# The third feed-forward block by Strassen's algorithm, with sums of weights made by adding transfers

## The chip, the core and the metric

The kernel runs on one core of a Trainium2 chip. A core has five engines that run side by side, each with its own queue of instructions, taken in order: TensorE (PE, matrix products into PSUM banks), VectorE (DVE), ScalarE (ACT), GpSimd (POOL) and SyncE (SP, which issues transfers). Sixteen DMA engines carry the transfers, whoever issues them. The metric is the device time of one execution in microseconds; 1209.74 us is the median of three runs before the change (1209.62 to 1209.84).

## The reference

The model is a decoder trunk of two layers on 256 tokens of width 1024, all in float32. Each layer is

```python
h = _swiglu(x, ffn_w1[l, 0], ffn_w3[l, 0], ffn_w2[l, 0])
x = _layernorm(ALPHA * x + 0.5 * h, ln_g[l, 0], ln_b[l, 0])
h = _mixer(x, ...)                      # gated position mixing and differential attention
x = _layernorm(ALPHA * x + h, ln_g[l, 1], ln_b[l, 1])
h = _swiglu(x, ffn_w1[l, 1], ffn_w3[l, 1], ffn_w2[l, 1])
x = _layernorm(ALPHA * x + 0.5 * h, ln_g[l, 2], ln_b[l, 2])
```

with `_swiglu(x, w1, w3, w2) = (silu(x @ w1) * (x @ w3)) @ w2`. So there are four feed-forward parts, two a layer; `w1` and `w3` have 1024 rows and 2816 columns each. The change touches only the products `x @ w1` and `x @ w3`.

## The kernel before, in words

**Split products.** TensorE multiplies in a rounded float32 format. To keep precision, every operand is split in two: a high part (`hi`, the rounded value, made by a copy on ScalarE) and a low part (`lo`, the rest, made by a subtraction on VectorE). A product of two split operands is three matmuls, x_hi w_hi, x_hi w_lo and x_lo w_hi (`three`, L256), added up in one PSUM bank. Weights come from memory unsplit: `stream` (L152) loads 128x2048 numbers (1 MB) into a buffer `raw` (L163, issued by SyncE) and splits it (L178 on ScalarE, L180 on VectorE) into buffers of 128x1024, `whi` and `wlo`. There are four `raw` buffers and eight each of `whi` and `wlo`, so loads and splits run ahead of TensorE by as much as these hold.

**Blocks of a feed-forward.** `ffn` (L599) takes the columns of `w1` and `w3` in five blocks of 512 columns each of w1 and w3 (block n = 0 to 4), by `gemm_b2` (L317); the rest of the columns goes by another function, and then comes the product with `w2`. In `gemm_b2` the 256 tokens are two halves of 128 (t = 0, 1), the 1024 rows of the weights two halves c of 512, and m is 0 for w1 and 1 for w3: four 1 MB buffers of weights, 2 x 2 x 8 x 3 = 96 matmuls of 128x128 by 128x512 into four banks. First all of the weights with the first half of the tokens, then all again with the second, so the split weights of a block stay until its second half. After each half of the tokens `done` makes silu(w1 part) times the w3 part (L612 on ScalarE, L613 on VectorE) into `planes`, and a background task transposes it: GpSimd parts it into two planes of 16-bit numbers (L193), SyncE issues a transposing transfer (L197), GpSimd joins the planes (L202), and ScalarE and VectorE split the result (L629, L631) for the product with `w2`.

**The norm at the start.** The first feed-forward of the kernel has its input ready (`gemm_first`). The other three start while the layer norm before them ends: the class `Norm` scales, transposes (L573 to L580) and splits the tokens half by half during block 0, finishes the token rows (L541) during block 1, and these three are the stages with `norm` set.

**What sets the order.** TensorE's order is the order in which the program is written; `beat` counts its work in units of 12 matmuls, and background tasks (`beside`) are woken when a count is reached; `front` (L605) gives for each block how many units after its start a transposition is issued. For the other engines a scheduler fixes the order when the program is built, by priorities (`step` raises the number with each load, `soon` lowers it) and with `behind`, which puts an instruction after another one. In the run each engine then takes its instructions strictly in that order.

Of the kernel before, what the change touches and what calls it, by code (L numbers as in the profile page):

```python
# [54 lines left out]
def trunk(ctx, tc, x, xT, w13a, w13b, w2, wb, wqk, wu, wg, wgr, wbr, wbrr, wo, gateb, gatebr, sgug, sgub, sguwT, sgubias, lam, diffg,  # L55
# [93 lines left out]

        return tc.issue_after(ins) if ins is not None else nullcontext()  # L150

    def stream(src, width=CH, sub=HC, lent=(), after=(None, None), pool=()):  # L152

        step()
        raw = raw_pool.tile([P, CH], F32, tag="raw", name=name("raw"))
        for g in gate:
            g[0] -= 1
        while len(gate) > 1 and gate[1][0] < 0:  # L160
            gate.pop(0)
        with behind(gate[0][1] if gate and gate[0][0] < 0 else None):
            loaded[0] = nc.sync.dma_start(raw[:, :width], src).ins  # L163
        out = []
        first = sooner.pop() if sooner else latest
        for o in range(0, width, HC):
            eng = G if o // HC in pool else V
            if o // HC in lent:
                hi, lo = ([act.tile([P, 512], F32R, tag="slot", name=name(n)) for _ in range(2)] for n in ("lhi", "llo"))
                at = [(hi[j], lo[j]) for j in range(2)]  # L170
            else:
                hi = hi_pool.tile([P, HC], F32R, tag="hi", name=name("whi"))
                lo = lo_pool.tile([P, HC], F32R, tag="lo", name=name("wlo"))
                at = [(hi[:, p : p + sub], lo[:, p : p + sub]) for p in range(0, HC, sub)]
            for p, (h, w) in zip(range(0, HC, sub), at):
                r = raw[:, o + p : o + p + sub]
                with behind(first[0]):
                    A.activation(h, r, AF.Copy)  # L178
                with behind(after[o // HC] or (first[1] if eng is V else None)):
                    eng.tensor_tensor(out=w, in0=r, in1=h.bitcast(F32), op=ALU.subtract)  # L180
            out.append((hi, lo))
        return out
# [134 lines left out]
    def gemm_b2(srcs, xh, xl, done, norm=None, second=(0, 1), each=None):  # L317
# [9 lines left out]
        for t in range(NT):  # L327
# [14 lines left out]
            with behind(latest[0] if t == 0 else None):  # L342
                done(t, ps[t])

    def gemm_first(srcs, done):

        step()
# [89 lines left out]
    class Norm:  # L437
# [5 lines left out]

        def __init__(self, l, i, scale, eps, after, last=False):
            self.scale, self.eps, self.last, self.done, self.front = scale, eps, last, set(), i
            self.ends, self.xhi, self.xlo = [None] * NT, {}, {}
            self.gT, self.bT = (v[:, l, i] for v in (ln_g, ln_b))
            self.y = x_tok
            self.group = 256 if last else 512
            self.st = [sm("st", D // self.group * 6, bufs=2) for _ in range(NT)]  # L450
            self.g, self.b = bc_load(lng[l, i], after), bc_load(lnb[l, i], after)
            if last:
                A.activation(self.g, self.g, AF.Copy, scale=-0.5)
                self.minus = s512("minus")
                A.activation(self.minus[:, :P], ident, AF.Copy, scale=-1.0)
                self.eps_t = self.minus[:, 2 * P : 2 * P + 1]
                V.memset(self.eps_t, eps)
                with behind(silu[0]):
# [85 lines left out]
        def sent(self):  # L544

            two = [s512("ntwo")]
            with behind(loaded[0]):
                gate.append([3, moved(self.via[0], two[0])])
            yield 0.2
            self.affine(0, 1, self.via[0], self.via[0], (2, 2), two[0])  # L550
            with soon():
                for h in range(2):
                    self.plane(A, 1, h, 0)
            yield 0.4
            two += [s512("ntwo") for _ in range(2)]
            for h in range(2):
                last = moved(self.via[1 + h], two[1 + h])
            gate.append([2, last])
            yield 0.7
            self.affine(1, 0, self.via[1], self.via[1], (1, 1, 2), two[1])  # L560
            yield 1.7
            self.affine(1, 1, self.via[2], self.via[2], (2, 2), two[2])

        def affine(self, t, h, src, xf, pieces, two=None):
            self.done.add((t, h))
            k = 0
            with soon():
                for n in pieces:
# [17 lines left out]
            if (t, h) == (1, 1):  # L586
                latest[:] = last
                sooner.append((self.xhi[0, 1], self.xlo[1, 0]))

        def ready(self, t, h):  # L590
            assert (t, h) in self.done, (t, h)
# [7 lines left out]
    def ffn(l, f, i, norm, last=False):  # L599
# [33 lines left out]
        for n in range(NB):  # L633
            srcs = [w13b[l, f, m * NB + n] for m in range(2)]
            if n == 0 and norm is None:
                gemm_first(srcs, front(n, (10.3, 10.3)))
            else:
                gemm_b2(srcs, xh, xl, front(n, (13.3, 10.3)), norm=norm if n == 0 else None)
        for j in range(FA, FT - 4, 2):
            for m, z in gemm_a2([w13a[l, f, j - FA + m] for m in range(2)], both, lambda m: t512("silu")):  # L640
                s = z[:, :T]
# [403 lines left out]
```

## Time and profile before

| | |
|---|---|
| median of three runs | 1209.74 us |
| span of the profiled execution | 1208.3 us |
| TensorE busy | 1202.6 us, 5891 matmuls |
| VectorE busy | 903.2 us |
| ScalarE busy | 719.9 us |
| GpSimd busy | 332.9 us |
| read from memory | 236.52 MB, 197 GB/s over the span |

The time of the profiled execution itself is its span, from the first to the last instruction; the median of the runs is 1.4 us above it. In rows of the timeline the first number is the start in us from the start of the span, the second the duration of the group, then engine, line, operation, what is written from what is read, the count, and in brackets how long the engine had been idle and what ended that. In rows by group, the numbers behind the bar are busy time in us, mean duration in ns, and idle time before with what ended it. In rows on transfers the last number is the median time in us from issue to landing.

### The profile page before, as it was taken

How to read it: one execution, taken by the hardware profiler on the slowest of the kernel's cores; microseconds unless marked ns; L12 is line 12 of the kernel's file. 1: busy time of each engine (PE TensorE's matmuls, PEld its weight loads, DVE VectorE, ACT ScalarE, POOL GpSimd, SP SyncE). 2: the span in 40 equal slices, each digit the busy share in tenths (PEclk: the TensorE clock that was granted, in tenths of full speed). 3: DMA queues.
4: the chain of work that ended last, by engine and by line, in shares of the span. 5: the costliest groups of instructions: out<-in, count | busy, mean ns of one | idle time of the engine just before them, and what ended most of it. 6: DMA issues, size and time to landing. Idle time of an engine off the chain costs nothing.

```text
span 1208.3 us, 16816 instructions
## 1 busy us (share of the span) xinstructions
PE 1202.6 (100%) x5891; PEld 1013.3 (84%) x5891; DVE 903.2 (75%) x1544; ACT 719.9 (60%) x1388; POOL 332.9 (28%) x442
## 2 busy tenths in 40 slices
PE   9999999999999999999999999999999999999998
PEld 8888888888888888888888888888888888888887
DVE  6686669897689886766686756688966989776763
ACT  6465547668855665554555554576788556564740
POOL 1433101256421234330053330004464012423300
PEclk9999999999999999999999999999999999999999
DMA  9967646768765666767476766476676764877540
GB/s 347 303 219 238 253 174 203 259 200 231 240 213 180 200 231 208 249 201 261 149 245 198 259 187 261 148 273 238 211 205 199 251 192 153 274 231 239 186 181 35
DMA packets 124006, 263.58 MB, mean 218 GB/s; under 512 B 88417, under 2 KB 89489, under 8 KB 97809
## 3 DMA queue, kind: packets, MB, share of 16 engines
q1 hardware_dynamic: 119664, 248.80, 62.0%
q0 software_dynamic: 3824, 13.18, 3.4%
q8 instruction: 46, 0.75, 0.3%
q10 hardware_dynamic: 432, 0.52, 0.1%
q14 instruction: 40, 0.32, 0.1%
HBM read 236.52 MB, written 1.05 MB: 197 GB/s over the span
## 4 chain that ended last, share of the span: by engine, by line
PE 99%; DMA 0%; DVE 0%; ACT 0%; issue 0%; ACTq 0%
PE bank L256 72%; PE bank L268 15%; PE bank L275 8%; PE bank L374 2%; PE sbank L704 1%; PE sbank L760 1%; PE sbank L878 1%; DMA xraw<-in_xT 0%; PE sbank L758 0%; PE sbank L533 0%; PE sbank L512 0%; DVE xtok L520 0%; ACT whi L220 0%; DVE st L471 0%; DVE xtok L467 0%; ACT x L220 0%
## 5 line engine op out<-in xcount | busy, mean ns | idle before, releaser
L180 DVE TENSOR_TENSOR wlo<-raw,whi 128x512 fp32r<-128x512 f32 (+1 forms) x566 | 524.6, 962 | 114.8 <-ACT whi L178 80.0
L178 ACT ACTIVATE whi<-raw 128x512 fp32r<-128x512 f32 (+1 forms) x570 | 433.3, 799 | 246.6 <-PE bank L256 183.0
L256 PE MATMUL bank<-whi,x 128*128 128x512 f32 x1480 | 460.7, 390 | 0.0
L256 PEld LDWEIGHTS bank<-whi,x 128*128 128x128 f32 x1480 | 277.9, 188 | 57.7
L256 PE MATMUL bank<-wlo,x 128*128 128x512 f32 x740 | 288.0, 389 | 0.0
L256 PEld LDWEIGHTS bank<-wlo,x 128*128 128x128 f32 x740 | 139.0, 188 | 28.2
L268 PE MATMUL bank<-x,whi 128*128 128x512 f32 x640 | 153.3, 391 | 0.0
L256 PE MATMUL bank<-whi,hhi 128*128 128x512 f32 (+1 forms) x374 | 141.2, 378 | 0.0
L256 PE MATMUL bank<-wlo,hhi 128*128 128x512 f32 (+1 forms) x374 | 141.0, 377 | 0.0
L256 PE MATMUL bank<-whi,hlo 128*128 128x512 f32 (+1 forms) x374 | 140.9, 377 | 0.0
L193 POOL COPY planes<-planes 128x512 uint16<-128x512 uint16 x80 | 87.1, 1116 | 193.9 <-DVE planes L613 193.9
L268 PEld LDWEIGHTS bank<-x,whi 128*128 128x128 f32 x640 | 118.2, 188 | 23.8
L202 POOL COPY planes<-planes 128x512 uint16<-128x512 uint16 x80 | 70.9, 931 | 95.8 <-DMA planes<-planes 95.5
L613 DVE TENSOR_TENSOR planes<-planes,bank 128x512 f32<-128x512 f32 x40 | 27.4, 684 | 83.8 <-issue 69.3
L612 ACT ACTIVATE planes<-bank 128x512 f32<-128x512 f32 x40 | 23.9, 598 | 102.6 <-PE bank L256 101.5
L275 PEld LDWEIGHTS bank<-x,wlo 128*128 128x128 f32 x640 | 81.4, 191 | 2.9
L275 PE MATMUL bank<-x,wlo 128*128 128x256 f32 x640 | 82.6, 283 | 0.0
L256 PEld LDWEIGHTS bank<-whi,hlo 128*128 128x128 f32 x374 | 70.4, 188 | 13.0
L256 PEld LDWEIGHTS bank<-whi,hhi 128*128 128x128 f32 x374 | 70.4, 188 | 12.8
L256 PEld LDWEIGHTS bank<-wlo,hhi 128*128 128x128 f32 x374 | 70.4, 188 | 12.6
L575 POOL COPY nvia<-ntwo 128x256 uint16<-128x256 uint16 x20 | 10.4, 565 | 198.1 <-DMA ntwo<-nvia 179.9
L680 POOL TENSOR_TENSOR swap<-swap,sin_t 128x512 f32<-128x512 f32 x16 | 27.1, 1695 | 100.0 <-DMA swap<-z 78.0
(209 smaller groups left out, 1392.0 us busy)
## 6 DMA issues: line engine op xcount, KB each, us to landing
raw<-in_w13b SPq DMA_DIRECT2D x76, 1024.0 KB, 5.8
raw<-in_w SPq DMA_DIRECT2D x40, 1024.0 KB, 6.2
raw<-in_wb SPq DMA_DIRECT2D x16, 1024.0 KB, 5.1
raw<-in_wqk SPq DMA_DIRECT2D x16, 1024.0 KB, 6.3
raw<-in_w13a SPq DMA_DIRECT2D x8, 1024.0 KB, 5.1
raw<-in_wgr SPq DMA_DIRECT2D x8, 1024.0 KB, 5.3
raw<-in_wg SPq DMA_DIRECT2D x8, 1024.0 KB, 5.0
raw<-in_wu SPq DMA_DIRECT2D x8, 1024.0 KB, 6.4
```

Source lines behind the costliest of these rows:

```text
L178: A.activation(h, r, AF.Copy)
L180: eng.tensor_tensor(out=w, in0=r, in1=h.bitcast(F32), op=ALU.subtract)
L193: G.tensor_copy(out=planes(out)[:, w], in_=numbers(src)[:, w])
L202: eng.tensor_copy(out=numbers(out)[:, w], in_=planes(src)[:, w])
L256: PE.matmul(ps, xx, w, start=start and n == 0, stop=stop and n == 2)
L268: PE.matmul(b[-1], hi[:, k * P : (k + 1) * P], xc(k), start=k == 0, stop=False)
L275: PE.matmul(b[n][:, :T], lo[:, k * P : (k + 1) * P], xc(k)[:, :T], start=False, stop=k == KT - 1)
L374: PE.matmul(ps[t][m], x[:, j, o + t * P : o + (t + 1) * P], y, start=k0 + j == 0 and o == 0 and y is hi, stop=k0 + j == KT - 1 and y is lo)
L612: silu[0] = A.activation(s, ps[0], AF.Silu).ins
L613: added[0] = V.tensor_tensor(out=s, in0=s, in1=ps[1], op=ALU.mult).ins
L680: turned_by[0] = G.tensor_tensor(out=s3, in0=s3, in1=s, op=ALU.mult).ins
L704: PE.matmul(banks[m][:, j * nk : (j + 1) * nk], rows(qT, m, j, t * P, P), rows(kT, m, j, 0, nk), start=True, stop=True)
```

## The change

In the three feed-forwards that have a norm in front of them, block n = 2 goes by `gemm_seven` in place of `gemm_b2`. The block's product is one of 2 x 2 parts: the tokens' rows t and the input's columns c for x, the weights' rows c and w1 or w3 for w. With w11, w21 the two row halves of w1's columns and w12, w22 those of w3's, Strassen's algorithm in a form with seven products gives both outputs. Four of the products take a sum or difference of x parts, which `Norm.seven` forms and splits on VectorE and ScalarE after the last part of x is ready, and keeps in buffers `sum`. Four products take a sum of weights: the loaded `raw` buffer is first split as it is, and then a transfer issued by GpSimd adds another part into it (`gather`, two halves of 512 KB, `accum_op`), from memory (w12) or from another `raw` buffer (w22, w21), and it is split again. Each product is 12 matmuls; partial results are copied out of their banks (`kept`) and put together on VectorE. `fetch` is the front of `stream`, made a function of its own. For block 1 the count to its transposition is smaller by one unit, since the block behind it has one unit less.

```diff
+    def pieces(raw):
+        out = []
+        for o in range(0, CH, HC):
+            hi = hi_pool.tile([P, HC], F32R, tag="hi", name=name("whi"))
+            lo = lo_pool.tile([P, HC], F32R, tag="lo", name=name("wlo"))
+            split(hi, lo, raw[:, o : o + HC])
+            out.append((hi, lo))
+        return out
+
+    def gather(out, src):
+        for o in range(0, CH, HC):
+            G.dma_start(out[:, o : o + HC], src[:, o : o + HC], accum_op=ALU.add)
+
+    def gemm_seven(srcs, sums, done):
+        x11, x12, x22 = ((lambda k, o, h=h, t=t: x_cat[h][:, k, o + t * P : o + (t + 1) * P])
+                         for t, h in ((0, 0), (0, 1), (1, 1)))
+        s1, s2, s3, s4 = (lambda k, o, v=v: v[bool(o)][:, k * P : (k + 1) * P] for v in sums)
+        bx, by, bz = (side_bank() for _ in range(3))
+
+        def product(ps, x, w, first):
+            for k in range(KT // 2):
+                hi, lo = (v[:, k % 2 * 512 : k % 2 * 512 + 512] for v in w[k // 2])
+                for n, (y, o) in enumerate(((hi, 0), (lo, 0), (hi, T))):
+                    PE.matmul(ps, x(k, o), y, start=first and k == n == 0, stop=k == KT // 2 - 1 and n == 2,
+                              skip_group_check=True)
+                beat(0.25)
+
+        def kept(ps):
+            v = s512("part")
+            A.activation(v, ps, AF.Copy)
+            return v
+
+        (w11, w21), (w12, w22) = ((s[:, :CH], s[:, CH:]) for s in srcs)
+        r11 = fetch(w11)
+        product(bx, x11, pieces(r11), True)
+        gather(r11, w12)
+        product(bz, s1, pieces(r11), True)
+        a, z = kept(bx), kept(bz)
+        r22 = fetch(w22)
+        gather(r11, r22)
+        product(bx, s2, pieces(r11), False)
+        b = kept(bx)
+        r12 = fetch(w12)
+        gather(r12, r22)
+        product(bz, s4, pieces(r22), False)
+        r21 = fetch(w21)
+        product(bx, s3, pieces(r12), False)
+        c = kept(bx)
+        gather(r11, r21)
+        product(by, x12, pieces(r21), True)
+        V.tensor_tensor(out=a, in0=by, in1=a, op=ALU.add)
+        V.tensor_tensor(out=b, in0=bz, in1=b, op=ALU.subtract)
+        done(0, (a, b))
+        V.tensor_tensor(out=c, in0=z, in1=c, op=ALU.subtract)
+        product(bx, x22, pieces(r11), False)
+        done(1, (bx, c))
...
+            if self.front:
+                yield 4
+                yield from self.seven()
...
+        def seven(self):
+            x11, x12, x21, x22 = (self.rows[v] for v in ((0, 0), (0, 1), (1, 0), (1, 1)))
+            self.sums = [slots("sum", 4, F32R) for _ in range(4)]
+            for v, (out, a, b, op) in zip((0, 2, 1, 3), ((x22, x21, x22, ALU.subtract), (x21, x11, x21, ALU.subtract),
+                                                         (x11, x22, x11, ALU.subtract), (x12, x12, x11, ALU.add))):
+                V.tensor_tensor(out=out, in0=a, in1=b, op=op)
+                split(*self.sums[v], out)
+                yield 1
...
             if n == 0 and norm is None:
                 gemm_first(srcs, front(n, (10.3, 10.3)))
+            elif n == 2 and norm:
+                gemm_seven(srcs, norm.sums, front(n, (10.3, 10.3)))
             else:
-                gemm_b2(srcs, xh, xl, front(n, (13.3, 10.3)), norm=norm if n == 0 else None)
+                early = norm is not None and n == 1
+                gemm_b2(srcs, xh, xl, front(n, (13.3 - early, 10.3 - early)), norm=norm if n == 0 else None)
```

(`self.rows` keeps the rows of x that `affine` was given, for `seven`. The loads, `fetch`, are as in `stream` before.)

More of the change, by code (lines that the diff above doesn't have):

```diff
@@ L150, in behind, with fetch @@
         return tc.issue_after(ins) if ins is not None else nullcontext()
-    def stream(src, width=CH, sub=HC, lent=(), after=(None, None), pool=()):
+    def fetch(src, width=CH):
         step()
@@ L163, in stream @@
             loaded[0] = nc.sync.dma_start(raw[:, :width], src).ins
+        return raw
+    def stream(src, width=CH, sub=HC, lent=(), after=(None, None), pool=()):
+        raw = fetch(src, width)
         out = []
@@ L445, in __init__ @@
             self.scale, self.eps, self.last, self.done, self.front = scale, eps, last, set(), i
-            self.ends, self.xhi, self.xlo = [None] * NT, {}, {}
+            self.ends, self.xhi, self.xlo, self.rows = [None] * NT, {}, {}, {}
             self.gT, self.bT = (v[:, l, i] for v in (ln_g, ln_b))
@@ L562, in sent @@
             self.affine(1, 1, self.via[2], self.via[2], (2, 2), two[2])
+            if self.front:
+                yield 4
+                yield from self.seven()
         def affine(self, t, h, src, xf, pieces, two=None):
             self.done.add((t, h))
+            self.rows[t, h] = xf
             k = 0
```

## The prediction

> **What bounds the kernel now.** I read the page first (busy shares, the granted clock, the chain that ended last), then the busy times of one feed-forward block, then by engine the timeline around that block, and last the transfers.
>
> ```profile
> PE 1202.6 (100%) x5891; PEld 1013.3 (84%) x5891; DVE 903.2 (75%) x1544; ACT 719.9 (60%) x1388; POOL 332.9 (28%) x442
> PEclk9999999999999999999999999999999999999999
> PE 99%; DMA 0%; DVE 0%; ACT 0%; issue 0%; ACTq 0%
> ...
> PE sbank L386 <- DVE warm L382: 1.1, 1, 1.1
> ...
> core 0: us, PE busy (x) PEld busy (x) DVE busy (x) ACT busy (x) POOL busy (x), PEclk, DMA share, GB/s
> ...
> 466.42:488.18 21.76, 21.76 (x97) 18.02 (x96) 14.10 (x23) 11.31 (x23) 6.59 (x8) 1.00 0.67 230
> ```
>
> TensorE is busy all the time, at full granted clock, and the chain is 99% TensorE: its longest wait, at the start, is 1.1 us. So a matmul taken away is worth its full slot, and any wait put in front of one costs its full length. The last row is the third block of the feed-forward after the first mixer: 96 matmuls in 21.76 us, 0.2267 us each. I call this the first stage; the second is the next feed-forward (third block from 646.87), the third is the last one (from 1063.87). Block starts come from the SiLU rows below: SiLU starts when the first rows' w1 part is complete, which is 12 matmuls (2.72 us) before the middle of a block, so the next block starts 13.60 us later: 452.82 + 13.60 = 466.42.
>
> ```profile
> 452.82 0.60 ACT L612 ACTIVATE planes<-bank 128x512 f32<-128x512 f32 x1 [7.01 <-PE bank L256]
> 456.90 1.15 ACT L178 ACTIVATE whi<-raw 128x512 fp32r<-128x512 f32 x2 [3.48 <-PE bank L256]
> 633.27 0.60 ACT L612 ACTIVATE planes<-bank 128x512 f32<-128x512 f32 x1 [7.01 <-PE bank L256]
> 637.35 1.15 ACT L178 ACTIVATE whi<-raw 128x512 fp32r<-128x512 f32 x2 [3.48 <-PE bank L256]
> 1050.27 0.60 ACT L612 ACTIVATE planes<-bank 128x512 f32<-128x512 f32 x1 [7.01 <-PE bank L256]
> ```
>
> The row at 456.90 is the other thing to see: ScalarE had waited 3.48 us for TensorE to give back a buffer of high parts. Weights lie ready and splitting runs only 466.42 - 456.90 = 9.5 us ahead of their use, because eight buffers of 1024 columns hold exactly one block. The change takes seven pairs of such buffers in turn, two per product at 2.72 us a product, so this lead of 9.5 us stays what each product has, and two steps that follow on each other's result must fit into it.
>
> **The gain.** Eight products of 12 matmuls become seven: 12 x 0.2267 = 2.72 us less per stage, 8.2 us in three (1201.6 us, the floor).
>
> **The new chain.** The buffer r11 is filled with w11, split for product 1, gets w12 added by transfer, is split for product 2, gets w22 added, is split for product 3. A transfer into r11 waits until both engines have read it, and a split waits until it has landed. Nothing lies between products 1, 2 and 3 on TensorE that could cover this. The adding transfers stand on GpSimd's queue, in the built order: both halves of w12+w22 (into r12), the two plane copies of block two, then the halves of r11+w12, then of r11+w22. So the first one, which waits for w12 to be loaded, holds up all the others. Rows for these steps:
>
> ```profile
> L180 DVE TENSOR_TENSOR wlo<-raw,whi 128x1024 fp32r<-128x1024 f32 x232 | 292.4, 1271 | 95.5 <-ACT whi L178 65.6 <-issue 23.7 <-PE bank L275 3.4
> L178 ACT ACTIVATE whi<-raw 128x1024 fp32r<-128x1024 f32 x232 | 241.5, 1057 | 139.1 <-PE bank L256 85.9 <-PE bank L268 42.9 <-DVE st L471 6.0
> L885 DVE TENSOR_TENSOR sgu<-sgu,u 128x512 f32<-128x512 f32 x8 | 5.5, 688 | 0.1
> L434 POOL DMA_DIRECT2D bc<-in_lng x6 | 3.4, 563 | 26.5 <-ACT whi L178 9.9 <-DVE hlo L631 8.4 <-DVE bc L433 8.1
> ...
> 448.12 0.33 SPq L163 DMA_DIRECT2D raw<-in_w13b  x1
> 453.83 1.23 SPq L197 DMA_TRANSPOSE planes<-planes  x1
> 455.15 0.53 SPq L163 DMA_DIRECT2D raw<-in_w13b  x1
> 629.42 1.23 SPq L197 DMA_TRANSPOSE planes<-planes  x1
> 1051.05 1.23 SPq L197 DMA_TRANSPOSE planes<-planes  x1
> ...
> 456.74 1.45 POOL L202 COPY planes<-planes 128x512 uint16<-128x512 uint16 x2 [1.55 <-DMA planes<-planes]
> 458.09 2.08 POOL L193 COPY planes<-planes 128x512 uint16<-128x512 uint16 x2
> 635.02 1.44 POOL L202 COPY planes<-planes 128x512 uint16<-128x512 uint16 x2 [2.81 <-DMA planes<-planes]
> ...
> raw<-in_w13b SPq DMA_DIRECT2D x76, 1024.0 KB, 5.8
> xtok<-in_x POOLq DMA_DIRECT2D x2, 512.0 KB, 4.3
> bc<-in_lnb POOLq DMA_DIRECT2D x6, 512.0 KB, 6.8
> q1 hardware_dynamic: 119664, 248.80, 62.0%
> q0 software_dynamic: 3824, 13.18, 3.4%
> ```
>
> One half is split in 1.06 + 1.27 = 2.33 us. No adding transfer is in the trace. Its price: plain transfers on GpSimd's queue use 3.4% of 1208.3 us for 13.18 MB, 1.6 us of all sixteen DMA engines per half (512 KB), and the quickest group lands in 4.3 us, so 2.7 us are fixed. Low end: an add moves like a plain copy, 1.6 us, landing in 4.3. High end: it reads its destination as well, twice the bytes, 3.3 us, landing in 6.0. I take the middle, 2.4 us, landing in 5.1, since the destination is read but written only once; the group that lands in 6.8 shows that other traffic can add as much again.
>
> The Trainium skill ("Collectives: The Full Stack", Part 3, on the bandwidth ceiling) says that a reducing transfer emits two read descriptors per chunk and so runs at half the copy rate. By that the high end is the value and the sum below would be that of the high end; no row here shows an adding transfer.
>
> First stage, on the clock of the profile. In the built order the load of w12 (448.12 before) stands behind the transposition of 453.83, so it goes out at 455.15 and lands 5.8 later, 460.95. GpSimd then issues the two adds into r12 (0.56 each) and copies planes for 2.08, and is free for r11+w12 at 464.2. The r12 halves land at 466.05 and 468.45; the r11 halves queue behind them: 470.85 and 473.25. Split: 473.2 and 475.6. TensorE wants the low part of product 2 at 466.42 + 2.72 + 0.23 = 469.37: 3.8 late. r11+w22: issued 473.2, landed 478.3, split 480.6; wanted at 466.42 + 5.44 + 0.23 = 472.09: 8.5 late. Second half: 475.6 + 5.1 + 2.33 = 483.0 against 472.09 + 1.36 + 8.5 = 481.95: 1.1 more, 9.6 in all (a half is 1.36 us of TensorE). Products 4 to 6 use buffers that landed long before. The add for product 7 goes out at 480.6 and 483.0 and is split by 490.5, wanted at 492.6: hidden by products 4 to 6, and if they were gone it would cost one more 7.4 us. The first load of block four takes the buffer of w22, free when product 4 is split (about 485), lands at 491, and block four starts at 495: hidden. Net 9.6 - 2.72 = +6.9 us.
>
> The DMA engines have room for this at the middle price: the row of the block shows them busy for 0.67 x 21.76 = 14.6 us, eight adding halves bring 19.2, and the block, now 28.6 us long, with the idle third of its neighbours (7 us each) holds the 33.8. At double price, 26.4, hardly.
>
> The third stage has the same distances (transposition at 1051.05, 12.8 us before its block, against 12.6): +6.9. In the second the transposition is at 629.42, 17.5 us ahead, so w12 lands at 636.55, when GpSimd has just become free (635.02 + 1.44). The r11+w12 halves then land at 646.45 and 648.85 behind the r12 ones, are split by 648.8 and 651.2 (wanted 649.8: in time), r11+w22 is split by 656.2 and 658.6 against 652.5 and 653.9: 4.7 late, net +2.0. Sum of the three: +15.8.
>
> **VectorE earlier on.** Forming four sums of x adds eight 0.69 us operations, half of them in front of the last splits of block two:
>
> ```profile
> 449.15 0.68 DVE L180 TENSOR_TENSOR wlo<-raw,whi 128x512 fp32r<-128x512 f32 x1
> ...
> 450.89 1.88 DVE L180 TENSOR_TENSOR wlo<-raw,whi 128x512 fp32r<-128x512 f32 x3
> ```
>
> These end at 452.77; four operations (2.75) and the reordered token products ahead of them move the first of the four to 453.6, wanted at 453.05. That is 0.5 us per stage, 1.5 in all (0 if VectorE catches up). ScalarE's extra copies of banks (three of 0.60) wait for TensorE and lie in its idle time.
>
> Sum: 15.8 + 1.5 = +17.3. The profiled execution has a span of 1208.3 us, 1.4 us under the median of 1209.74; on the median I get 1227. Ends by the same timetable: plain-copy price +2.9, -2.2, +2.9 and nothing for VectorE, 1213; double price +11.3, +6.5, +11.3 and 1.5, 1240.
>
> **Rivals.** *Faster.* The place is r11+w22 before product 3. If w12 is loaded as soon as its buffer is free (so that GpSimd's adds to r11 go out at 461.5), everything hangs on the landing time G of one half: the wait is 461.5 + 2G + 4.66 - 472.09, and it is under the 2.72 us gained when G is under 4.3. With r12 behind the transposition G must be under 3.0. For it:
>
> ```profile
> L865 POOL DMA_DIRECT2D wsT<-in_sguwT x4: 561/600/640, 337.9 to 936.0; - x4
> ...
> DMA to landing us min/median/max: 3.4/6.8/10.2
> ```
>
> The quickest landing on this queue is 3.4 us (256 KB). At that value the first and third stage gain 1.8 each and the second its 2.7: 1203.5. Against it: the medians of 4.3 to 6.8.
>
> *VectorE becomes the bound, the transfers are hidden.* The block's splits go from 8 to 14 halves, 6 x 1.27 more, and three bank sums of 0.69: 14.10 + 9.7 = 23.8 us against 19.04 of TensorE. If none of it finds room in the idle 7.66 us that the row of this block shows, each stage is 23.8 - 21.76 = 2.0 us longer: 1216. Against it: neighbouring blocks have idle VectorE time.
>
> *The clock falls.* If TensorE's clock is halved for some 3.4 us after each wait as long as those above (3.8 and 8.5 - 3.8 = 4.7 in the first and third stage, 3.7 in the second), each costs 1.7, five in three stages 8.5: 1235. No wait of the trace before is long enough to test it (longest 1.1). The Trainium skill ("TensorE: Matmul & The Clock Gate", Part 1) has this rule, with an idle window of about 3.4 us before the clock halves; no run here shows it.
>
> **How the numbers follow.** The measurement tells about 0.2% (2.4 us) from no change. An add priced between plain and double, VectorE included (1213 to 1241): 0.64, with 1227 in it. Beyond that, double price with the clock's fall or traffic on top: 0.13. Within 0.2%: 0.08, plain price and the second stage's gain nearly cancelling. Faster: 0.15, almost all by the early load and quick landings. So slower 0.77. The range 1206 to 1246 leaves out the quicker part of the faster case and the end of the slow one, two in ten together.
>
> **What would show it.** Right: TensorE waits for wlo from a raw buffer that waits for a software-queue transfer, at products 2 and 3 of each of the three stages, more in the first and third; the adds into r12 issued only after w12 landed; adding halves landing in 5 us or more; 36 matmuls fewer. Wrong: halves landing under 4 us, w12 loaded before the transposition, or TensorE still at 100% with waits elsewhere.

## The result, and the profile after

The changed kernel takes 1254.98 us (median of four runs, 1253.78 to 1259.35), the kernel before 1209.79 beside it: a ratio of 1.038, with an interval of 1.0368 to 1.0393. The forecast was 1227, slower but within 1246. The direction was right, the size was not: the span grew by 44.4 us (1208.3 to 1252.7) where the forecast's sum was 17.3.

From the page after: busy time by engine, granted clock by slice, the queue of the software transfers, and the adding transfers from SBUF.

```profile
PE 1217.2 (97%) x5855; PEld 1010.3 (81%) x5855; DVE 945.0 (75%) x1571; ACT 747.0 (60%) x1406; POOL 369.4 (29%) x466
PEclk9999999999999997999998999999999999989999
q0 software_dynamic: 7280, 25.76, 8.6%
raw<-raw POOLq DMA_DIRECT2D x18, 512.0 KB, 4.6
```

There are 36 matmuls fewer, as meant, and yet TensorE is busy 14.6 us longer and idle for 35 us. The clock row has three dents, one in each stage.

The whole loss lies in the three stages. I cut a stage from the SiLU of block one's first half to that of block four's, the same work in both kernels. Busy times in these stretches, before and then after (columns: stretch and length, then busy us of PE, PEld, DVE, ACT and POOL with counts, granted clock, DMA share, GB/s):

```profile
452.82:518.10 65.28, 65.28 (x289) 54.05 (x288) 44.02 (x64) 33.32 (x64) 23.18 (x29) 1.00 0.73 234
633.27:698.55 65.28, 65.28 (x289) 54.05 (x288) 44.26 (x65) 33.34 (x64) 21.71 (x26) 1.00 0.75 231
1050.27:1115.55 65.28, 65.28 (x289) 54.07 (x288) 43.80 (x64) 33.33 (x65) 24.13 (x30) 1.00 0.74 235
```

```profile
452.39:535.17 82.78, 69.87 (x277) 53.49 (x277) 57.52 (x73) 41.16 (x69) 35.17 (x35) 0.92 0.83 226
650.30:728.33 78.03, 69.78 (x277) 52.17 (x276) 57.90 (x72) 41.05 (x68) 31.47 (x34) 0.96 0.87 240
1080.01:1159.69 79.68, 71.56 (x277) 54.56 (x277) 59.98 (x75) 41.28 (x68) 31.63 (x32) 0.91 0.84 232
...
466.54:500.62 34.08, 24.12 (x86) 18.05 (x85) 20.41 (x22) 18.18 (x26) 7.78 (x11) 0.80 0.92 196
500.62:535.17 34.55, 32.01 (x133) 24.25 (x133) 28.57 (x41) 18.99 (x39) 18.93 (x18) 1.00 0.89 280
```

The stages grew by 17.5, 12.75 and 14.4 us, 44.65 together. The last two rows cut the first stage once more: the third block (seven products, 19.0 us of matmuls at full clock) takes 34.1 us, the rest behind it 34.6.

How a chain of sums looks in the first stage, from the timeline:

```profile
457.99 1.24 SPq L202 DMA_TRANSPOSE planes<-planes  x1
...
445.58 10.40 POOL L207 COPY planes<-planes 128x512 uint16<-128x512 uint16 x2 [4.42 <-DMA planes<-planes]
465.09 1.81 POOL L363 DMA_DIRECT2D raw<-raw  x2 [2.83 <-issue]
467.38 2.38 POOL L363 DMA_DIRECT2D raw<-in_w13b  x2
478.38 0.85 POOL L363 DMA_DIRECT2D raw<-raw  x1 [8.62 <-DMA raw<-in_w13b]
...
475.77 1.06 ACT L225 ACTIVATE whi<-raw 128x1024 fp32r<-128x1024 f32 x1 [16.13 <-DMA raw<-in_w13b]
...
476.88 0.79 PE L381 MATMUL sbank<-whi,sum 128*128 128x512 f32 x1 [7.46 <-ACT whi L225]
484.46 0.50 PE L381 MATMUL sbank<-whi,sum 128*128 128x512 f32 x1 [1.76 <-ACT part L387]
```

ScalarE stands idle for 16.13 us until r11+w12 has landed; TensorE waits 7.46 for that at product 2, and then 1.76 at product 3, for a copy of product 1's bank (`part`) that stands on ScalarE behind the first split of r11+w22. The next transfer in GpSimd's queue, the first half of r11+w22, went out at 478.38, after 8.62 us in which GpSimd waited for r11+w12. Short stretches of the same time show the rate and the clock:

```profile
463.00:465.00 2.00, 2.00 (x11) 1.65 (x10) 0.00 (x0) 0.00 (x0) 0.00 (x0) 1.00 1.03 430
472.00:476.00 4.00, 0.00 (x0) 0.00 (x0) 0.00 (x0) 0.23 (x1) 0.00 (x0) 0.50 1.03 201
477.00:482.00 5.00, 4.53 (x10) 3.18 (x11) 3.76 (x5) 2.59 (x6) 2.00 (x4) 0.50 0.55 109
483.00:485.00 2.00, 0.50 (x1) 0.19 (x1) 1.87 (x4) 1.41 (x2) 0.00 (x0) 1.00 0.99 197
```

With plain loads (first row) the DMA engines, all busy, move 430 GB/s; with adding transfers (second and last) they are as busy at about 200. And TensorE's clock is at one half during the wait and for the five microseconds of work behind it: the matmul at 476.88 takes 0.79 us, not 0.39.

What TensorE waited for in all (us, times, longest):

```profile
PE sbank L381 <- ACT whi L225: 9.7, 2, 7.5
PE bank L261 <- DVE wlo L185: 7.9, 9, 2.6
PE sbank L381 <- ACT part L387: 6.2, 4, 2.6
PE sbank L381 <- DVE wlo L227: 4.2, 8, 0.8
```

### The profile page after: what moved, and what is told of

It reads as the page before. It is cut to its first block, busy times and chain, and to the rows that moved or that the text cites. A ratio compares the mean times of both kernels' runs of the same rounds, so it can differ in the third digit from the quotient of the medians.

```text
span 1252.7 us, 16871 instructions
## 1 busy us (share of the span) xinstructions
PE 1217.2 (97%) x5855; PEld 1010.3 (81%) x5855; DVE 945.0 (75%) x1571; ACT 747.0 (60%) x1406; POOL 369.4 (29%) x466
## 5 line engine op out<-in xcount | busy, mean ns | idle before, releaser
L185 DVE TENSOR_TENSOR wlo<-raw,whi 128x512 fp32r<-128x512 f32 (+1 forms) x518 | 499.2, 1000 | 103.5 <-ACT whi L183 71.2
L183 ACT ACTIVATE whi<-raw 128x512 fp32r<-128x512 f32 (+1 forms) x522 | 405.6, 815 | 227.3 <-PE bank L261 150.9
L261 PE MATMUL bank<-whi,x 128*128 128x512 f32 x1288 | 403.2, 391 | 0.0
L261 PEld LDWEIGHTS bank<-whi,x 128*128 128x128 f32 x1288 | 242.7, 188 | 49.4
L261 PE MATMUL bank<-wlo,x 128*128 128x512 f32 x644 | 254.3, 395 | 9.1 <-DVE wlo L185 7.9
L261 PEld LDWEIGHTS bank<-wlo,x 128*128 128x128 f32 x644 | 121.2, 188 | 44.0 <-DVE wlo L185 20.0
L207 POOL COPY planes<-planes 128x512 uint16<-128x512 uint16 x80 | 88.5, 1153 | 123.9 <-DMA planes<-planes 123.9
L198 POOL COPY planes<-planes 128x512 uint16<-128x512 uint16 x80 | 85.3, 1119 | 121.2 <-DVE planes L697 121.2
L227 DVE TENSOR_TENSOR wlo<-raw,whi 128x1024 fp32r<-128x1024 f32 (+1 forms) x58 | 60.4, 1074 | 47.3 <-ACT whi L225 46.6
L225 ACT ACTIVATE whi<-raw 128x1024 fp32r<-128x1024 f32 (+1 forms) x58 | 52.0, 936 | 54.7 <-DMA raw<-in_w13b 31.5
L696 ACT ACTIVATE planes<-bank 128x512 f32<-128x512 f32 x34 | 20.3, 597 | 64.8 <-PE bank L261 47.0
```

The source lines that it names most:

```text
L198: G.tensor_copy(out=planes(out)[:, w], in_=numbers(src)[:, w])
L207: eng.tensor_copy(out=numbers(out)[:, w], in_=planes(src)[:, w])
L225: a = A.activation(hi, src, AF.Copy).ins
L227: return a, eng.tensor_tensor(out=lo, in0=src, in1=hi.bitcast(F32), op=ALU.subtract).ins
L261: PE.matmul(ps, xx, w, start=start and n == 0, stop=stop and n == 2)
L696: silu[0] = A.activation(s, ps[0], AF.Silu).ins
```

## The experiments

Three numbers sum up each kernel, in us over the three stages: *ahead* (SiLU of block one's first half to the start of the third block), *third block* (first to last matmul of the seven products) and *behind* (to the SiLU of block four). They are cut from TensorE's rows, and can be off by half a microsecond a stage where records are missing. The time of the changed kernel is the median of four runs and that of the reordered products of two; every other is a single run, so a difference of two or three microseconds between two rows says little. *Ahead* and *third block* are best read together: a stage whose third block starts late gives the sums more time.

| kernel | time | ahead | third block | behind |
|---|---|---|---|---|
| changed kernel | 1255.0 | 46.1 | 92.6 | 101.9 |
| no sums of weights | 1206.3 | 44.8 | 57.6 | 89.7 |
| plain copies for sums | 1237.3 | 46.2 | 73.7 | 102.1 |
| w12+w22 queued later | 1255.9 | 45.8 | 95.8 | 99.9 |
| products reordered | 1265.1 | 43.1 | 117.6 | 89.8 |
| sums on GpSimd | 1256.5 | 42.6 | 107.4 | 92.4 |
| first sum on VectorE, rest on GpSimd | 1247.3 | 42.2 | 93.5 | 96.9 |
| the same, bank copies first | 1249.8 | 41.4 | 93.5 | 100.9 |
| clock held by useless matmuls | 1249.2 | 50.5 | 94.4 | 89.9 |
| w12 loaded first | 1251.2 | 42.2 | 89.0 | 105.6 |
| bank copies first | 1252.6 | 49.8 | 87.8 | 101.1 |
| w12 loaded and bank copies first | 1249.1 | 42.2 | 92.2 | 100.8 |
| without w12+w22 | 1248.9 | 48.7 | 82.0 | 103.3 |
| without r11+w22 | 1246.5 | 50.8 | 87.6 | 93.4 |
| sums in quarters | 1245.5 | 49.7 | 87.7 | 94.3 |
| first sum on VectorE, rest by transfers | 1240.7 | 42.3 | 83.3 | 101.1 |
| the same in quarters | 1231.6 | 42.5 | 70.6 | 102.9 |
| last sum in w21's buffer | 1288.0 | 46.1 | 132.1 | 95.2 |
| all these together | 1256.7 | 42.2 | 103.8 | 95.8 |

### Are the sums of weights the cause?

```diff
     def gather(out, src):
         for o in range(0, CH, HC):
-            G.dma_start(out[:, o : o + HC], src[:, o : o + HC], accum_op=ALU.add)
+            pass                                                                    # no sums
+            G.dma_start(out[:, o : o + HC], src[:, o : o + HC])                     # plain copies
```

(The two added lines belong to two kernels.) No sums:

> All adding transfers are left out: the same seven products, splits and sums of x, but r11 and r12 are split again as they are, so the output is not the reference's. Theory (the lost time is the chain of adding transfers, with the waits, the falling clock and the late loads it brings): the 2.72 us per stage show, less about 0.5 for VectorE, so 1202 to 1205. Rival (VectorE and ScalarE are the bound through six more split halves, three bank sums and four sums of x): still 1216 or more.

Plain copies:

> The transfers of gather stay, on the same queue and of the same size, but copy instead of adding, so the output is not the reference's. Theory (waiting in GpSimd's queue and behind one another is what costs, not the addition): halves land only a little sooner, 1240 to 1255. Rival (the addition itself, reading the destination as well, is what costs): landings fall by a third or more and the time is 1225 or less.

Without sums: 1206.3, a clock of 1.00 throughout, and 63.0 us in the undisturbed stages (13.9 ahead, 19.2, 29.95). So all that the seven products ask of TensorE, ScalarE and VectorE fits, and the rival that VectorE becomes the bound is out. Of the 8.2 us hoped for 3.2 arrive against the kernel before beside it (1209.56): VectorE is late once (2.8 us), and an undisturbed stage is 2.3 us shorter and not 2.7. These 63.0 us are what the other kernels are measured against. The third block of the last stage and the part behind it, without sums:

```profile
1062.71:1081.92 19.21, 19.21 (x86) 15.93 (x85) 19.21 (x25) 16.69 (x28) 7.18 (x4) 1.00 0.75 233
1081.92:1111.87 29.95, 29.95 (x133) 24.80 (x133) 23.46 (x35) 15.22 (x30) 20.77 (x17) 1.00 0.86 289
```

Plain copies: 1237.3, between the two forecasts. Waiting for transfers costs 31 us even if they only copy, and the addition another 18. The copies' rows:

```profile
raw<-raw POOLq DMA_DIRECT2D x18, 512.0 KB, 2.8
q0 software_dynamic: 7280, 25.76, 6.1%
```

A half lands in 2.8 us in place of 4.6. The queue used 3.4% of 1208.3 us before, so 24 halves cost 75.4 - 41.1 = 34.3 us of all DMA engines as copies, 1.43 each, and 107.7 - 41.1 = 66.6 as sums, 2.78 each: double. The rule of the Trainium skill cited in the prediction ("Collectives: The Full Stack", Part 3) agrees with that rate.

### Does the order of the sums, or of the products, matter?

```diff
-        gather(r12, r22)
+        gather(r12, r22, last)      # in GpSimd's queue behind the last transfer of r11+w22
```

> The adds into r12 are put behind both adds of r22 into r11 in GpSimd's queue; nothing else changes. Theory (the first add waits for w12's load and holds up the chain of r11): r11+w12 is issued some 3 us sooner and lands within 5 to 6 us instead of 8 to 11, the wait at product 2 falls from 7.5 to about 3 us, some 4 to 5 us per stage with the clock: about 1240. Rival (the chain of r11 itself is what costs, its place in the queue nothing): 1252 to 1257.

It was 1255.9, no change: the third block became 3.2 us longer, the part behind it 2 shorter. The sum that had been held up, r11+w12, was issued at 464 in the first stage, but the waits moved on to later products (TensorE's waits for `part`, 6.2 us before, are 11.3). The second kernel keeps this and gives the chain more room:

```diff
-  w11, w11+w12, w11+w12+w22, w22, w12+w22, w21, last     (order of the products' weights)
+  w11, w21, w11+w12, w22, w11+w12+w22, w12+w22, last
```

> As the kernel with the r12 adds behind, and the products in another order: w11, then w21 (own bank), w11+w12, w22, w11+w12+w22, w12+w22, last; so one product lies in front of the second link of the chain and two in front of the third. Theory (waits of TensorE at the links of the chain): the wait at w11+w12 is gone, that at the third link about 1 us, a new one of about 4 us at w12+w22, whose add now comes last; 1215 to 1225. Rival (VectorE and ScalarE are the bound): no better than with the adds behind alone, about 1240.

It was slower, 1265.1 (ratio 1.0459, 1.0428 to 1.0489). The waits, and the end of the one in the first stage (ScalarE's timeline, then TensorE's):

```profile
PE sbank L383 <- ACT part L389: 41.2, 9, 11.6
```

```profile
488.37 1.06 ACT L225 ACTIVATE whi<-raw 128x1024 fp32r<-128x1024 f32 x1 [0.95 <-DMA raw<-raw]
489.33 0.58 ACT L389 ACTIVATE part<-sbank 128x512 f32<-128x512 f32 x1
...
489.96 0.79 PE L383 MATMUL sbank<-whi,sum 128*128 128x512 f32 x1 [10.95 <-ACT part L389]
```

TensorE waits for a bank to be copied out (`part`), a copy of 0.58 us; that copy stands on ScalarE behind splits which themselves wait for sums. The bank had been full since 479. My expectation had looked at the sums' distances and not at ScalarE's queue.

### Adding on an engine

```diff
-            G.dma_start(out[:, o : o + HC], src[:, o : o + HC], accum_op=ALU.add)
+            eng.tensor_tensor(out=out[:, o : o + HC], in0=out[:, o : o + HC], in1=src[:, o : o + HC], op=ALU.add)
```

with w12 loaded ahead of product 1 and kept; `eng` is GpSimd, or VectorE for the first sum.

> The four sums of weights of each stage are made by GpSimd's tensor_tensor in place of adding transfers; w12 is loaded once, as the second load, and kept. Theory (the loss comes from the adding transfers, which fill the DMA engines at half rate): no adding traffic is left, the DMA share of the stages falls from 0.83-0.87 to about 0.7, and what remains is eight additions of 128x1024 by some 3 us (the 128x512 ones of GpSimd took 1.29 to 1.71 us) behind the copies of the turned planes: 66 to 72 us a stage, 1215 to 1230 in all. Rival (the loss is the chain of dependent sums and splits, whoever adds): 78 us a stage or more, over 1240.

> As the kernel with the sums on GpSimd, but the first sum (w11+w12), for which the second product waits, on VectorE (1.25 us a half). Theory: the second product no longer waits for GpSimd's queue; 64 to 69 us a stage, 1207 to 1222. Rival (VectorE, 57 us busy in a stage of 63, becomes the bound): slower than the kernel with all four on GpSimd.

No adding traffic is left and they are no better: 1256.5 and 1247.3. Again it is ScalarE's order (25.8 us of waits for `part` in the second). So the order was mended, in this kernel and in two with transfers:

```diff
-        product(bx, s2, pieces(r11), False)
-        b = kept(bx)
+        p3 = pieces(r11, with_a)          # split behind the copy of product 1's bank
+        z = kept(bz)
+        product(bx, s2, p3, False)
+        b = kept(bx)                      # and so on for the later ones
```

> The kernel with the first sum on VectorE and the others on GpSimd, with the bank copies ahead of the splits on ScalarE. Theory (in that kernel the sums were in time and ScalarE's order alone held TensorE, 25.8 us of waits for part): the waits go, 64 to 68 us a stage, 1207 to 1220. Rival (the sums of GpSimd, 3 us a half, or VectorE's splits hold TensorE): over 1230.

> The changed kernel with another order on ScalarE alone: each copy of a bank (part) stands ahead of the next sum's splits, and block four's splits behind the last of them. Theory (ScalarE's queue, in which bank copies stand behind splits that wait for a sum, makes part of the loss): the waits for part, 6.2 us in three stages, go, and with them the half clock behind them: 1244 to 1250. Rival (adding transfers alone decide): the waits turn up again at the splits, within 3 us of 1255.

> Adding transfers from SBUF alone (w12 loaded ahead of the first product) with the bank copies ahead of the splits. Theory (adding transfers set the stage; ScalarE's order adds little here, since no wait for part was left in the kernel with w12 loaded first): 1243 to 1251. Rival (ScalarE's order is the larger half of the loss in this kernel too): under 1235.

The waits for `part` went in all three, and the time hardly changed: 1249.8 (after 1247.3), 1252.6 (after 1255.0) and 1249.1 (after 1251.2). In the first of them the wait merely has another name; waits of TensorE, then VectorE's timeline, then GpSimd's:

```profile
PE sbank L383 <- DVE wlo L227: 22.0, 6, 6.0
```

```profile
470.68 7.74 DVE L723 TENSOR_TENSOR hlo<-planes,hhi 128x256 fp32r<-128x256 f32 x4
...
465.71 11.68 POOL L363 TENSOR_TENSOR raw<-raw,raw 128x1024 f32<-128x1024 f32 x4
```

While GpSimd adds (3 us a half), four VectorE operations of 128x256, 0.41 us each in the changed kernel's median, take 1.9 each. So GpSimd is no place for the sums beside a VectorE that is busy 57 us of a stage, and these kernels do not show what sums that cost nothing else would give.

### The clock

```diff
+        held(24)      # matmuls of no use, into the bank that product 6 begins anew
         product(bz, s1, pieces(r11), True)
...
+        held(12)
         product(bx, s2, pieces(r11), False)
```

> The changed kernel, with 24 matmuls of no use ahead of the second product and 12 ahead of the third (into the bank of the sixth product, which is begun anew), so that TensorE is busy through most of the two waits. Theory that the fall of the clock is part of the loss: the granted clock of the stages rises from 0.91-0.96 to over 0.97 and each stage gains 2 to 4 us, 1243 to 1249. Rival (the fall is no loss, since what follows waits for the transfers anyway): the clock rises and the time stays within 2 us of 1255.

The clock of the stages rose to 0.98 and the time fell by 5.7 us, to 1249.2. From short stretches of the changed kernel, busy time times the missing clock is 4.0, 2.8 and 4.1 us in the three third blocks and 1.6 ahead of the last one, 12.5 us. But the table does not show the 5.7 us as a part of these: ahead and third block together did not become shorter (144.9 against 138.7), and the gain lies behind (89.9 against 101.9), where a longer third block alone can bring it, as shown below. The useless matmuls also take 5.4 and 2.7 us of TensorE in each stage, and no wait is left behind them at products 2 and 3 but one of 0.8, so they may have held these products up themselves. So 12.5 us is what the slow clock added to TensorE's work; how much shorter the kernel would be at full clock is not shown, since what follows a slow product may be another wait.

### Chain or traffic?

```diff
-        gather(r12, r22)      # left out in one kernel
-        gather(r11, r22)      # left out in another
```

> The sum w12+w22 is left out (product 5 takes w12 alone, so its result is not the reference's): two of the eight adding halves of a stage, off the chain of r11. Throughput theory: 2 halves of 2.7 us of all DMA engines less a stage, 4 to 5.5 us: 1238 to 1243. Chain theory: r11's sums wait for one another as before: 1250 to 1256.

> The sum (w11+w12)+w22 is left out (products 3 and 7 take other weights, so the result is not the reference's): as many adding halves as the sum w12+w22, but a link of the chain of r11. Throughput theory: as without w12+w22, 1238 to 1243. Chain theory: a link of some 9.7 us (4.5 for the sum, 1.06 and 1.25 for the splits, 2.5 for the second half, half a us of issue) against a product of 5.4 goes, with the slow clock behind it: 5 to 8 us a stage, 1231 to 1240, and 10 us or more below the kernel without w12+w22.

```diff
-        for o in range(0, CH, HC):
-            G.dma_start(out[:, o : o + HC], src[:, o : o + HC], accum_op=ALU.add)
+        for o in range(0, CH, 512):
+            G.dma_start(out[:, o : o + 512], src[:, o : o + 512], accum_op=ALU.add)
```

> Each sum by four adding transfers of 128x512 in place of two of 128x1024, and the splits as wide: same bytes, shorter links, 24 more issues of 0.85 us on GpSimd. Chain theory: a quarter lands in some 3 us, a link is 4 us shorter: 1241 to 1248. Throughput theory: within 3 us of 1255, or slower by the issues.

The first two gave 1248.9 and 1246.5, 2.4 apart where the chain theory wanted ten, and less than the 12 to 17 that traffic alone wanted: neither pure theory holds. (The second expectation also has a product at 5.4 us; it is 12 x 0.2267 = 2.72, so the chain theory should have wanted still more.) Where the time went is of more use. Without r11+w22, ahead and third block together are as long as in the changed kernel (138.4 against 138.7): TensorE now waits 13.2 us for `part`, longest (3.05 us in the first stage, 3.64 in the second) behind the split of the last sum, r11+w21, and the splits that follow it; all of the gain lies behind the block. Without w12+w22 they are 8.0 us shorter. So here a link taken out of the chain handed its wait to a later sum. In the quarters (where the splits are narrower too) the bytes are the same, the queue's share is larger, and the time is 9.5 us shorter.

```profile
raw<-raw POOLq DMA_DIRECT2D x36, 256.0 KB, 4.1
q0 software_dynamic: 10736, 25.76, 9.2%
```

So the amount of traffic alone is not what sets these stages. But only 1.3 of the 9.5 us are won ahead of and in the third block (137.4) and 7.6 behind it, so the quarters do not show that the rest is r11's chain. And traffic is close behind: 0.83 x 82.78 = 68.7 us of all DMA engines in the first stage after, 67.9 and 66.9 in the others, against 47.7 to 49.0 before. A stage was 65.28 us. By these figures a stage with all its sums made by transfers could hardly have become shorter than before even with every wait gone, unless part of the transfers moved out of it; no run here tests that.

Shortening the first link in other ways: w12 loaded ahead and added from SBUF, and then that sum by VectorE with the other three by transfers and the bank copies first, as halves and as quarters.

> w12 is loaded ahead of the first product and stays; the first adding transfer takes it from SBUF in place of a second read from memory. Theory (the DMA engines' throughput and the 8.7 us landing from memory set the second product's wait): the first sum lands in 4.5 us, 4 us earlier a stage, and 1 MB less is moved: 1238 to 1246. Rival (the chain of the later sums sets the stage's end, so an earlier first sum only moves the wait): within 3 us of 1255.

> w12 loaded first and its sum into r11 by VectorE (two of 1.25 to 1.6 us), the other three sums by adding transfers from SBUF, bank copies ahead of the splits. Both theories: six adding halves a stage and the first link 3 us shorter; 1232 to 1243 (against 1249 with all four by transfers in the same order). Rival (VectorE, slowed in the first block, is late instead): 1247 or more.

> As the kernel with the first sum on VectorE and the rest by transfers, with those in quarters of 128x512 and the splits as wide. If the gains add (14.2 and 9.5 below 1255): 1229 to 1234. If the wait only moves on to the next sum: 1237 to 1242. Behind the third block, where w11's buffer is still held, 33 to 34 us of the stage are left either way, against 29.9 without sums.

They took 1251.2, 1240.7 and 1231.6. The gains add up: the first sum on VectorE, with the bank copies first, brings 14.2 us and the quarters 9.1 more. The third blocks go from 92.6 to 83.3 and 70.6 us in all, against 57.6 without sums, and in the last kernel TensorE's clock is back at 0.98 to 1.00. This is the best kernel with all its sums, and it is still 22 us slower than the kernel before.

### Behind the third block

Of the three stages' excess 12.2 us lie behind the third block, where block four's loads are late. SyncE's timeline of the changed kernel:

```profile
490.24 2.60 SPq L161 DMA_DIRECT2D raw<-in_w13b  x2
492.94 1.31 SPq L202 DMA_TRANSPOSE planes<-planes  x1
494.78 0.64 SPq L161 DMA_DIRECT2D raw<-in_w13b  x1
495.47 4.48 SPq L202 DMA_TRANSPOSE planes<-planes  x1
500.06 9.71 SPq L161 DMA_DIRECT2D raw<-in_w13b  x3
```

```diff
-        gather(r11, r21)
-        product(by, x12, pieces(r21), True)
+        product(by, x12, pieces(r21), True)
+        gather(r21, r11)                       # product 7 then takes r21
```

> The last sum is written into w21's buffer (after its splits) and not into the first one, so the first buffer, which block four's first load takes, is free some 4 us earlier. Theory (block four starves because that buffer is held): the time from the end of the third block to the stage's end falls from 34.5, 34.4 and 33.0 us towards the 29.9 of the kernel without sums: 1245 to 1250. Rival (those loads are late by their place behind the transpositions and by the traffic): within 3 us of 1255.

> Together: w12 loaded first and its sum on VectorE, the other sums by transfers of 128x512 from SBUF, the splits as wide, bank copies ahead of the splits, the last sum in w21's buffer. If the gains add (14.2 of the first three, 9.5 of the quarters, 5 of the buffer): 1224 to 1232. If they are the same chain bought twice: 1234 to 1242. Under 1209 only if the chain is then shorter than the products.

1288.0 and 1256.7, outside all that was expected of either. Behind the third block 6.7 us were won, about half of what the first expectation allowed, but the third block became 39.5 us longer: the last sum is now made while two of block four's loads and a transposition run, and TensorE waits for it 7.5 to 13.7 us a stage.

```profile
PE sbank L381 <- ACT whi L225: 43.2, 5, 13.7
...
DMA to landing us min/median/max: 4.4/8.1/17.5
```

(The first row is of TensorE's waits, the second of the adding transfers.) A longer third block also gives block four's loads more time by itself: in the kernels with reordered products and with the clock held the part behind is 29.9 a stage without any change to its buffers. So it stays open how much of the 12.2 us is the held buffer and how much the place of the loads behind the transpositions and the last adding transfers.

## Why the prediction was wrong, point by point

**What was forecast and what was measured,** in us over three stages; the clock's part is taken out of its row and shown by itself. The measured column divides up the time that the stages took; it does not say what each part would bring if it alone were gone:

| term | forecast | measured |
|---|---|---|
| gain of 36 matmuls | -8.2 | -6.8 (3 x 63.0 against 195.84) |
| waits in the third blocks | 9.6 + 4.7 + 9.6 = 23.9 | 10.9 + 7.6 + 5.6 = 24.1 |
| VectorE ahead of them | 1.5 | 2.8 |
| clock | 0 in the sum; a rival, 8.5 | 10.9 + 1.6 = 12.5 |
| behind them, block four | 0, "hidden" | 12.2 |
| sum | 17.3 | 44.8 |

**The chain was right in place and mechanism, its stages were not.** The place (products 2 and 3, for a raw buffer that waits for a software-queue transfer) and the mechanism (split, sum, split of r11, with GpSimd's queue blocked) came out as worked out. That the sum of the waits agrees to 0.2 is luck: the first and second stage waited longer than forecast and the third less, though it was to wait as long as the first. There product 2 waited no longer than 0.76 us at a time, and the wait of 2.60 at product 3 was for a bank copy on ScalarE behind the split of r11+w22; ScalarE's queue had no place in the timetable. The price taken for an adding half was 2.4 us of the DMA engines and 5.1 to land; it is 2.78, and 4.4 to 4.7 alone, 7.5 to 11.2 behind others. Of GpSimd's copies ahead of the transposition one pair had taken 6.25 us before (the row here), and one took 10.40 in the first stage after, so the transposition and w12's load behind it went out at 457.99 and 459.39, 4.2 later than the timetable had them.

```profile
447.55 6.25 POOL L193 COPY planes<-planes 128x512 uint16<-128x512 uint16 x2 [5.95 <-DVE planes L613]
```

In the third stage after, they took 2.01, and instead VectorE was late in block one:

```profile
1072.40 2.01 POOL L207 COPY planes<-planes 128x512 uint16<-128x512 uint16 x2 [3.83 <-DMA planes<-planes]
...
1082.76 0.80 PE L261 MATMUL bank<-wlo,x 128*128 128x512 f32 x1 [2.56 <-DVE wlo L185]
```

**First step that failed: "the first load of block four [...] hidden".** The timetable followed only the first of the four loads, to 485 against a block four at 495. It went out at 490.24, as late as the block itself, but the third and fourth, behind two transpositions, at 494.78 and 500.06. The part behind the third block took 12.2 us more than without sums, in three stages.

**Second step that failed: the clock stood in a rival and not in the sum.** The rival had five falls at 1.7 us each. There were five, of 3.4 to 10.2 us, and each made TensorE's work 1.7 to 4.1 us longer. It was given a small chance on the ground that no wait before was long enough to test it; by the counts in the last section, waits of 3.7 to 4.7 us bring the fall nearly always, so the sum had to hold it or give it even odds. The first step alone would have left the sum inside the range (17.3 + 12.2 = 29.5, which is 1239); with the measured size of both it is 17.3 + 12.2 + 12.5 = 42.0, near the 44.4 measured. What is left is VectorE's 1.3 and the gain's 1.4. This is an account and no test: no run has full clock and the same waits, so what the clock alone costs stays open.

**The rivals.** VectorE as the bound: refuted by the kernel without sums. Faster by quick landings: a half lands in no less than 4.4 us, 0.1 over the point from which it was to decide, and only with w12 loaded early, which was not so. The clock: true, beside the chain and not in place of it. The range's end, 1246, held double price or the clock, but not both with block four.

## What to carry to other kernels

Saving matmuls pays only if the operands of the new ones are there without a detour. A sum made by transfer costs a round of landing and splitting (here 4.5 + 1.06 + 1.25, some 7 us a half, against 2.72 for a whole product), and such rounds in a chain put TensorE to waiting in every order tried here. Before such a change, follow each link in the timetable through to the block behind it, every load and not only the first, and give the slow clock a place in the sum behind each wait of two microseconds or more. Read the built order of every engine that has a wait in it: 0.58 us of bank copies on ScalarE, behind splits that waited, held TensorE for 41 us in one of these kernels.

## What the runs showed that I had not expected

- *The clock falls early, but not always.* In the first stage TensorE's last matmul before the wait ended at 469.42 and the clock was at one half from 471.7, 2.3 us later; it came back after 5 us of work. A wait of 2.56 us in the third stage brought 3.2 us at half clock (the row below), while one of 2.8 in the kernel without sums brought none. The Trainium skill ("TensorE: Matmul & The Clock Gate", Part 1) gives an idle window of about 3.4 us, and says that the window runs freely, so that where in it the work lands decides. The scatter agrees with that; the falls after 2.3 to 2.6 us are earlier than a full window. The record of the granted clock in the traces shows the grid: within each of the twenty, every stretch at half clock begins a whole multiple of 3.41 us after the others and, unless the trace ends first, lasts 3.41, 6.83 or another multiple. Counting TensorE's idle time by the windows of that grid (from the matmul rows, at full clock), all 70 windows with 1.97 us or more were followed by half clock, none with less than 1.25 was, and of the 49 between 11 were. The wait of 2.8 us without a fall was cut by an edge of the grid into 1.7 and 1.1.

```profile
1082.80:1086.00 3.20, 3.20 (x8) 2.50 (x9) 3.17 (x5) 0.34 (x1) 1.65 (x3) 0.50 0.24 100
```

- *VectorE and GpSimd take turns being late.* In block one VectorE runs without a gap once it forms the sums of x. Then either a pair of GpSimd's copies takes 8 to 10.8 us in place of 2, or VectorE itself is late by 2.6 to 2.8 us; in the stages of the changed kernel and of the one with plain copies that I looked at it was one of the two. The Trainium skill ("SBUF — State Buffer", "SBUF: two separate sides") says that a VectorE operation with two inputs in SBUF and a GpSimd operation that reads SBUF exclude each other for a whole instruction. These rows agree, and so do VectorE's operations of 0.41 us that took 1.9 beside GpSimd's additions.
- *Adding transfers suffer from others more than loads do.* In the kernel with the last sum in w21's buffer a 512 KB half of that sum took 9.9 to 17.5 us to land beside loads and a transposition, against 4.4 alone; the 1 MB loads issued in the same stretches took 4.9 to 11.3.
